# A hybrid encoder layer on one core: the branch product's sums and low halves on VectorE only, the second branch's blocks all ahead of the first branch, two pairs interleaved, the out product opened over seven of eight blocks

## The chip, the cores and the metric

The kernel runs on one core of one Trainium2 chip. The metric is the device time of one execution in microseconds; lower is better. The core's engines are TensorE (PE), VectorE (DVE), ScalarE (ACT), GpSimd (POOL) and SyncE (SP); here SP issues nearly all DMAs, and POOL those that add to memory.

## The reference

One layer of a streaming encoder over 1024 prompt rows and 32 sample rows, in float32. Only the piece between the two branches and the residual is touched: `oa` (1056 rows of 1024) and `ob` (1056 rows of 512) come from the two attention branches, `ga` and `gb` are gates.

```python
h = rms_norm(x, g_pre_mix)
qa, ka, va, ra, alr, qb, kb, vb, ga, gb = split_cols(h @ w_in)
oa, s_gla = gla_branch(qa, ka, va, ra, alr, w_a2, b_a2, g_gla, gla_s0, gla_block)
ob, k_rows, v_rows = attn_fn(qb, kb, vb, rel_bias)
mix = (jax.nn.sigmoid(ga) * (oa @ w_br_a) + jax.nn.sigmoid(gb) * (ob @ w_br_b)) @ w_out
x = x + rms_norm(mix, g_post_mix)
...
```

## The kernel before

Everything is held transposed: a tile has 128 feature rows and up to 1056 tokens (1024 of the prompt and 32 of the sample). The tokens are cut into three chunks of 352 (`chunk(c)`) or two halves of 528 (`one`, `two`). The weights are cut into blocks of 128 by 128.

A product keeps float32 accuracy by splitting each operand into a high half (a copy by ACT into a shorter format) and a low half (the operand less its high half, a subtraction). Each block is then three matmuls: high times high, weight's high times low, weight's low times high. `split_hi_lo` and `split_both` issue the copy on ACT and the subtraction on DVE; `branch_half` does this for half a weight tile (four blocks, 128x512), with the subtraction on POOL (line 1684).

The branch product has two kinds of units. A **branch B unit** (`branch_b(n, c)`) is block n of `ob @ w_br_b` for one chunk, 12 matmuls of 352 columns (lines 231 to 233); its eviction multiplies by the gate row `gb[n]` (line 1721) and the last chunk stores the row to `d_tb[n]`. A **branch A product** (`branch_a(m, n)`) is one of seven products by which a pair m of output blocks (m and m+4) over two halves of inner blocks and two halves of tokens is formed with seven products in place of eight: `a11, s0, s1, s3, s2, a12, a22`, each 24 matmuls of 264 columns (lines 1816 to 1818). Their moving operands are the rows of `oa` or sums of them: `b11`, `b21`, `b22` are parts of the rows and `t1` to `t4` sums, made once by `first_sum` and `third_sum` (POOL) and `t2_sum` and `t4_sum` (DVE) and split by the functions with `_split`. All four pairs use the same operands, so they are made during the first pair. A product accumulates in one of four PSUM pairs `BK`; evictions copy (ACT), add and gate (DVE), and POOL's DMA adds the finished rows to `d_tb` in memory (`add_row`).

The order is the list `seq`: branch B's blocks 4, 5 and 6 (blocks 0 to 3 ran earlier), then pair after pair of branch A with the next pair's a11 ahead of a pair's a12, and branch B's block 7 at the end. The table `work` says which sums and splits are issued with which unit, `at` splits a unit's weights two units ahead. Weights are loaded by SP (`weights_load`, two buffers of two halves each). Rows of gates and products (`ev`) rotate through four buffers (`evt`), so a load into one waits for the store from it to land. PE, DVE and ACT run in the order in which the code issues; POOL's and SP's queues too.

Then `mix @ w_out` opens: rows of `d_tb` are loaded into `ml`, split into `mh` and `ml` (`mix_split`, `mix_last`), and each output block sums eight row blocks in the order `MIX = (0, 4, 1, 5, 2, 6, 3, 7)`. Rows 3 and 7 come straight from the last pair's eviction and from branch B's last block.

Of the kernel before, what the change touches and what calls it, by code (L numbers as in the profile page):

```python
# [18 lines left out]
P = 128  # L19
# [91 lines left out]
B21P = ()  # L111
B22P = ()


def emit(tc, a):
# [1427 lines left out]
    for u in range(16):  # L1543
# [81 lines left out]
        if u == 14:  # L1625
            while fill["at"] < 3 * FIRST:
                piece()
                flush()
            xp.release()
            key_copies(15)  # L1630
            bo = pool("bo", side="right")
            for x in "hl":
                OB[x] = tl(bo, [P, 4, T], F32R, tag="b" + x)
            eb = pool("eb", side="right")
            branch_split(0)
            split_tile()
            load_tile()
            gate_rows(1)
# [31 lines left out]
    XO = {n: [[t[:, h] for t in oa[r + k]] for k in range(HK)] for n, r, h in (("b11", 0, one), ("b21", HK, one), ("b22", HK, two), ("t4", 0, two))}  # L1670
# [4 lines left out]
    def split_both(n, k, t, eng=ve):  # L1675
        ac.activation(XO[n][k][0], t, AF.Copy)
        eng.tensor_tensor(XO[n][k][1], t, XO[n][k][0], op=ALU.subtract)

    wsp = {}

    def branch_half(key, t, eng=po):
        h, l = wsp[key] = [tl(wp, [P, HK, P], F32R, tag=x, bufs=4) for x in ("whi", "wlo")]
        ac.activation(h, t, AF.Copy)
        eng.tensor_tensor(l, t, h, op=ALU.subtract)
# [26 lines left out]
    def branch_b(n, c):  # L1711
        h, l = [t[n % 2] for t in FB] if n < 6 else wsp["b", n]
        s = chunk(c)
        ps = (BK[1 + c % 2][:, 0] if BK else ps_two()[:, 0] if (n, c) == (6, NC - 1) else ps_mm())[:, : s.stop - s.start]
        product(ps, [h], [l], [(k, k) for k in range(HK)], lambda k: OB["h"][:, k, s], lambda k: OB["l"][:, k, s])

        def evac():
            if n == 6 and c == 0:
                gb[n] = evt()
            g = gb[n]  # L1720
            ve.tensor_tensor(g[:, s], ps, (oa[KT - 1][0].bitcast(F32) if n == 6 else g)[:, s], op=ALU.mult)
# [31 lines left out]
    def third_sum(k):  # L1753
        t = thirds[k] = tl(sx, [P, HT], tag="t", bufs=1)
        po.tensor_tensor(t, raw_row(HK + k)[:, two], raw_row(k)[:, two], op=ALU.subtract)

    def b22_split(k):
        split_both("b22", k, raw_row(HK + k)[:, two], po if k in B22P else ve)

# [6 lines left out]
    def b21_split(k):  # L1766
        split_both("b21", k, raw_row(HK + k)[:, one], po if k in B21P else ve)

# [3 lines left out]
    def half_tile():  # L1772
        return tl(sx, [P, HT], tag="n", bufs=4)
# [6 lines left out]
    def pair_load(m):  # L1780
        q = pairs_[m] = Pair()
        q.m, q.x, q.v, q.w = m, BK[0 if m % 2 else 3], BK[2], BK[1]
        q.g = [evt() for i in range(2)]
        q.parts = [t[:, h] for t in (evt(), evt()) for h in (one, two)] if m == 0 else []
        for i in range(2):
            dma.dma_start(q.g[i], d_ga[m + HK * i])
# [20 lines left out]
    def branch_a(m, n):  # L1807
        q = pairs_[m]
# [12 lines left out]
        def evac():  # L1821
            if n in ("a11", "s0", "s1"):
                t = q.parts.pop(0) if q.parts else half_tile()
                setattr(q, n, t)
                ac.activation(v2(t), V if n == "s0" else X, AF.Copy)
            elif n == "s3":
                ve.tensor_tensor(v2(q.s1), V, v2(q.s1), op=ALU.add)
                gated_part(q, 0, two, v2(q.s1), 1)
            elif n == "s2":
                ve.tensor_tensor(v2(q.s0), X, v2(q.s0), op=ALU.add)  # L1830
                gated_part(q, 1, two, v2(q.s0), -1)
            elif n == "a12":
                ve.tensor_tensor(v2(q.a11), W, v2(q.a11), op=ALU.add)
                gated_part(q, 0, one, v2(q.a11), 1)
                if m < HK - 1:
                    add_row(q, 0)
            else:
                gated_part(q, 1, one, X, -1)
                if m < HK - 1:
                    add_row(q, 1)  # L1840
# [4 lines left out]

    def mix_load(c):
        for k in MIX[:-2]:
            dma.dma_start(ml[:, k, chunk(c)].bitcast(F32), d_tb[k, :, chunk(c)])

    def mix_split(k, c):  # L1850
        s = chunk(c)
        split_hi_lo(mh[:, k, s], ml[:, k, s], ml[:, k, s].bitcast(F32))

    def mix_last(n, c):
        s = chunk(c)
        g = pairs_[HK - 1].g[n // HK][:, s]
        ve.tensor_tensor(g, g, (gb[n] if n == KT - 1 else tv)[:, s], op=ALU.add)
        split_hi_lo(mh[:, n, s], ml[:, n, s], g)

    def terms():  # L1860
        tr = pool("tr")
        for n in ("t1", "t2", "t3"):
            XO[n] = [[tl(tr, [P, HT], F32R, tag=f"{n}{k}{x}") for x in "hl"] for k in range(HK)]
        return tr
# [6 lines left out]
    use = {("b", 6): 6, ("b", KT - 1): len(seq) - 3} | {u: i for i, u in enumerate(seq) if u[0] != "b"}  # L1871
# [5 lines left out]
    def split_weights(u):  # L1877
        i = order_w.index(u)
        if i % 2 == 0:
# [4 lines left out]
    work = {0: [(first_sum, 0), (first_sum, 1), (first_split, 0)], 1: [(first_sum, 2), (first_split, 1)], 2: [(first_sum, 3), (first_split, 2)], 3: [(first_split, 3)],  # L1884
            4: [(t1_split, 0)], 5: [(t1_split, 1), (t1_split, 2)], 6: [(t1_split, 3), (t2_sum, 0)], 7: [(third_sum, 0), (t2_sum, 1), (t2_split, 0)],
            8: [(t2_sum, 2), (t2_split, 1), (t3_split, 0), (third_sum, 1)], 9: [(t2_sum, 3), (t2_split, 2), (t2_split, 3), (t3_split, 1), (third_sum, 2)],
            10: [(b22_split, 0), (b22_split, 1), (t3_split, 2), (third_sum, 3), (b22_split, 2)],
            11: [(b22_split, 3), (t3_split, 3), (t4_sum, 0), (b21_split, 0)], 12: [(t4_sum, 1), (b21_split, 1)],
            13: [(t4_sum, 2), (b21_split, 2)], 14: [(t4_sum, 3), (b21_split, 3), (t4_split, 0), (t4_split, 1)], 15: [(t4_split, 2), (t4_split, 3)]}
    tr = mp = None  # L1890
# [3 lines left out]
    def out_halves(n, eng):  # L1894
        raw = tl(wp, [P, KT, P], tag="raw", bufs=2)
        dma.dma_start(raw, a["w_out"][n])
        for i in range(2):
            branch_half(("out", n, i), raw[:, i * HK : i * HK + HK], eng)
            if i == 0:
                yield  # L1900
# [3 lines left out]
    out0, out1 = out_halves(0, po), out_halves(1, ve)  # L1904

    work |= {N - 4: [(mix_split, 0, 0), (mix_split, 4, 0)], N - 3: [(next, out0), (next, out0), (mix_split, 1, 0), (mix_split, 5, 0)],
             N - 2: [(mix_split, 2, 0), (mix_split, 6, 0), (mix_last, HK - 1, 0)], N - 1: [(next, out1)]}
    for i, u in enumerate(seq):
        if i == 4:
            tr = terms()  # L1910
        if i == 9:
            repsum((0, 0, 4))
            BK = [ps_pair() for x in range(4)]
            pair_load(0)
        evac = branch_b(*u[1:]) if u[0] == "b" else branch_a(u[1], u[0])
        if u[0] == "s3":
            if u[1] + 1 < HK:
                pair_load(u[1] + 1)
            else:
                gb[KT - 1], tv = evt(), evt()  # L1920
                dma.dma_start(gb[KT - 1], d_gb[KT - 1])
                dma.dma_start(tv, d_tb[HK - 1])
        if u == ("a22", HK - 1):
            tr.release()
            op.release()
# [3 lines left out]
            for c in range(NC):  # L1929
                mix_load(c)  # L1930
# [4 lines left out]
        if u[0] == "s2":  # L1935
            pair_gate(u[1])
        evac()
    next(out1)
    sx.release()
# [162 lines left out]

    for c in range(NC):
# [3 lines left out]
        for n in range(KT):  # L2107
            hi, lo = wout[n]
            ps = ps_mm()
            product(ps[:, :CW], hi, lo, [(k, k) for k in MIX], lambda k: mh[:, k, s], lambda k: ml[:, k, s])  # L2110
            if c == 0:
                if n == 0:
                    out_weights(2)
                if n < 2:
                    mix_last(HK - 1, 1 + n)
                    mix_last(KT - 1, 1 + n)
                if n == 1:
                    ev.release()
                    bo.release()
# [1008 lines left out]
```

## Time and profile before

| what | us |
|---|---|
| median of 3 runs (lowest, highest) | 1884.36 (1881.78, 1886.1) |
| the profiled execution's own time | 1884.82 |
| span of its records | 1883.1 |
| first matmul of branch B's block 4 | 880.50 |
| first matmul of branch A | 897.98 |
| first matmul of the out product | 999.22 |

Lines of the profile name an engine, a line of the kernel, an operation, its output and input tiles, and the shape. A wait row reads: engine, the waiting tile and line, what released it, the total, the number and the longest. In a timeline the brackets hold the idle time just before an operation and what ended it.

### The profile page before, as it was taken

The page shows a single profiled execution, that of the slowest core. Times are in us where ns is not written, and L with a number is a line of the kernel's source. Part 1 is how long each engine was busy: PE and PEld are TensorE (multiplying, and loading weights), DVE is VectorE, ACT ScalarE, POOL GpSimd, SP SyncE. Part 2 cuts the span into 40 slices and gives each one's busy share as a digit, 9 for nine tenths or more (in the row PEclk, how much of TensorE's full clock was granted, in tenths as well). Part 3 has the DMA queues.
Part 4 walks back from the last instruction along what each step waited for, and adds up shares of the span by engine and source line. Part 5 has one row for each costly group of instructions (what it writes and reads, how often), then busy time and mean ns, then how long its engine had stood idle before and what let it go on. Part 6 is the DMA issues. An engine that isn't in the chain of part 4 may idle for free.

```text
span 1883.1 us, 35213 instructions
## 1 busy us (share of the span) xinstructions
PE 1847.1 (98%) x13808; PEld 1810.0 (96%) x13808; DVE 1278.7 (68%) x2387; ACT 974.8 (52%) x2062; POOL 285.7 (15%) x466
## 2 busy tenths in 40 slices
PE   8999999999999999999899999999999999999997
PEld 8999999999999999999899999999999999999996
DVE  6955543666655766776736776888888876558777
ACT  7545334666666666553525455433333355555555
POOL 0000001131100111102540111111122210000112
PEclk9999999999999999999999999999999999999998
DMA  7222326355534657578575467555557679887746
GB/s 281 84 103 104 114 81 200 96 144 136 124 82 124 171 134 191 166 221 299 166 208 196 143 246 286 182 173 182 177 165 184 165 204 303 279 287 240 237 151 110
DMA packets 129618, 336.00 MB, mean 178 GB/s; under 512 B 15204, under 2 KB 40620, under 8 KB 128812
## 3 DMA queue, kind: packets, MB, share of 16 engines
q1 hardware_dynamic: 92732, 220.74, 35.8%
q0 software_dynamic: 35280, 108.34, 21.9%
q10 hardware_dynamic: 1440, 4.69, 0.6%
q8 instruction: 108, 1.77, 0.4%
q14 instruction: 58, 0.48, 0.1%
HBM read 225.98 MB, written 132.75 MB: 191 GB/s over the span
## 4 chain that ended last, share of the span: by engine, by line
PE 36%; DVE 4%; issue 4%; DMA 3%; ACT 2%; POOL 1%; SPq 0%; POOLq 0%; DVEq 0%; ACTq 0%
PE two L2357 6%; PE two L2355 6%; PE two L2356 6%; PE two L2802 3%; PE two L2800 3%; PE two L2801 3%; PE mm L233 2%; PE mm L231 2%; PE mm L232 2%; DMA raw<-in_w_br_a 1%; PE two L2264 1%; DMA uraw<-d_b 1%; PE two L2266 1%; PE two L2265 1%; DMA d_tb<-ev 0%
## 5 line engine op out<-in xcount | busy, mean ns | idle before, releaser
L824 PE MATMUL mm<-xh,whi 128*128 128x352 f32 x696 | 238.1, 342 | 1.0 <-ACT ev L715 1.0
L826 PE MATMUL mm<-xh,wlo 128*128 128x352 f32 x696 | 225.0, 323 | 0.0
L825 PE MATMUL mm<-xl,whi 128*128 128x352 f32 x696 | 224.6, 323 | 0.0
L2802 PE MATMUL two<-d,wlo 128*128 128x264 f32 x616 | 174.4, 283 | 1.1 <-DVE wlo L2536 1.1
L2801 PE MATMUL two<-d,whi 128*128 128x264 f32 x616 | 174.7, 284 | 0.2 <-DVE d L2487 0.2
L2800 PE MATMUL two<-d,whi 128*128 128x264 f32 x616 | 174.6, 284 | 0.0
L2345 ACT ACTIVATE whi<-ws 128x512 fp32r<-128x512 f32 x88 | 55.5, 631 | 162.0 <-PE two L2356 155.4
L824 PEld LDWEIGHTS mm<-xh,whi 128*128 128x128 f32 x696 | 131.2, 189 | 3.7 <-ACT ev L715 1.3
L825 PEld LDWEIGHTS mm<-xl,whi 128*128 128x128 f32 x696 | 131.2, 189 | 0.3
L826 PEld LDWEIGHTS mm<-xh,wlo 128*128 128x128 f32 x696 | 130.6, 188 | 0.0
L2356 PE MATMUL two<-ml,whi 128*128 128x264 f32 x448 | 126.5, 283 | 0.0
L2357 PE MATMUL two<-mh,wlo 128*128 128x264 f32 x448 | 125.9, 284 | 0.0
L2355 PE MATMUL two<-mh,whi 128*128 128x264 f32 x448 | 125.8, 283 | 0.0
L2802 PEld LDWEIGHTS two<-d,wlo 128*128 128x128 f32 x616 | 116.4, 189 | 1.6 <-DVE wlo L2536 1.6
L2801 PEld LDWEIGHTS two<-d,whi 128*128 128x128 f32 x616 | 115.8, 188 | 0.5 <-DVE d L2487 0.5
L2800 PEld LDWEIGHTS two<-d,whi 128*128 128x128 f32 x616 | 115.7, 188 | 0.0
L961 ACT ACTIVATE s<-s,sm 128x640 f32<-128x640 f32 (+5 forms) x72 | 50.6, 703 | 93.3 <-DVE sm L960 90.5
L237 DVE TENSOR_TENSOR wlo<-raw,whi 128x512 fp32r<-128x512 f32 x80 | 55.8, 702 | 57.5 <-ACT whi L236 52.2
L619 PE MATMUL two<-th,whi 128*128 128x264 f32 x320 | 90.8, 284 | 0.0
L620 PE MATMUL two<-tl,whi 128*128 128x264 f32 x320 | 90.8, 284 | 0.0
L621 PE MATMUL two<-th,wlo 128*128 128x264 f32 x320 | 90.6, 284 | 0.0
L2536 DVE TENSOR_TENSOR wlo<-wraw,whi 128x512 fp32r<-128x512 f32 (+1 forms) x81 | 51.7, 643 | 50.7 <-ACT whi L2535 50.5
(784 smaller groups left out, 6357.9 us busy)
## 6 DMA issues: line engine op xcount, KB each, us to landing
raw<-in_w_in SPq DMA_DIRECT2D x52, 512.0 KB, 3.7
d_b<-av POOLq DMA_DIRECT2D x33, 528.0 KB, 3.5
d_ws<-in_w_down POOLq DMA_DIRECT2D x24, 704.0 KB, 6.6
uraw<-d_b SPq DMA_DIRECT2D x32, 528.0 KB, 5.2
raw<-in_w_up SPq DMA_DIRECT2D x29, 512.0 KB, 4.6
sraw<-in_w_up SPq DMA_DIRECT2D x22, 512.0 KB, 3.6
wraw<-d_ws SPq DMA_DIRECT2D x16, 704.0 KB, 5.7
d_b<-sm POOLq DMA_DIRECT2D x11, 792.0 KB, 6.3
```

What stands on the lines that cost most here:

```text
L619: pe.matmul(ps[:, j, :HC], w[0][:, k], x[0](k, s), start=st, stop=False, skip_group_check=True)
L620: pe.matmul(ps[:, j, :HC], w[0][:, k], x[1](k, s), start=False, stop=False, skip_group_check=True)
L621: pe.matmul(ps[:, j, :HC], w[1][:, k], x[0](k, s), start=False, stop=sp_, skip_group_check=True)
L824: pe.matmul(ps, wh, h[:, k, s], start=(k == 0), stop=False)
L825: pe.matmul(ps, wh, l[:, k, s], start=False, stop=False)
L826: pe.matmul(ps, wl, h[:, k, s], start=False, stop=(k == cnt - 1))
L2355: pe.matmul(ps[:, j, :HC], w[0][:, k], x[0][:, k, s], start=st, stop=False, skip_group_check=True)
L2356: pe.matmul(ps[:, j, :HC], w[0][:, k], x[1][:, k, s], start=False, stop=False, skip_group_check=True)
L2357: pe.matmul(ps[:, j, :HC], w[1][:, k], x[0][:, k, s], start=False, stop=sp_, skip_group_check=True)
L2800: pe.matmul(o, wh, xh_[:, s], start=(k == 0 and p in (0, 4, 5)), stop=False, skip_group_check=True)
L2801: pe.matmul(o, wh, xl_[:, s], start=False, stop=False, skip_group_check=True)
L2802: pe.matmul(o, wl, xh_[:, s], start=False, stop=(k == HD - 1 and p in (3, 4, 6)), skip_group_check=True)
```

## The change

It moves all sums and all low halves of the branch product to DVE; POOL keeps only the DMAs that add to `d_tb`. Branch B's block 7 follows block 6, so that all branch B units stand ahead of branch A; its gate row is loaded at block 6's first eviction. Pairs 0 and 1 of branch A are interleaved, then pair 2 begins inside pair 1's end and pair 3 inside pair 2's; the gate rows of a pair are loaded at the units in `LOADS`, and the sigmoid on them moves from the eviction of s2 to that of s3. Tiles move between pools: the sums' halves get buffers of their own, and six half tiles take the products' parts. Chunk 0 of the rows 0, 4, 1, 5, 2, 6 is loaded into staging tiles during the last pair, and its splits stand around the last product. The first two blocks of the out product each run over seven row blocks, and then the eighth is added to both.

```diff
+            eb = pool("eb", side="right")
             bo = pool("bo", side="right")
...
-            eb = pool("eb", side="right")
...
-    sx = pool("sx", side="right")
-    op = pool("op", side="right")
+    tr = pool("tr")
+    T1 = {n: [[tl(tr, [P, HT], F32R, tag=f"{n}{k}{x}") for x in "hl"] for k in range(HK)] for n in ("t1", "t2", "t3")}
+    op = pool("op")
+    sx = pool("sx")
...
-    def branch_half(key, t, eng=po):
+    def branch_half(key, t):
         h, l = wsp[key] = [tl(wp, [P, HK, P], F32R, tag=x, bufs=4) for x in ("whi", "wlo")]
         ac.activation(h, t, AF.Copy)
-        eng.tensor_tensor(l, t, h, op=ALU.subtract)
+        ve.tensor_tensor(l, t, h, op=ALU.subtract)
...
         def evac():
             if n == 6 and c == 0:
-                gb[n] = evt()
-            g = gb[n]
-            ve.tensor_tensor(g[:, s], ps, (oa[KT - 1][0].bitcast(F32) if n == 6 else g)[:, s], op=ALU.mult)
-            if n == KT - 1:
-                if c == 0:
-                    mix_last(n, 0)
-            elif c == NC - 1:
-                dma.dma_start(d_tb[n], g)
+                gb[6], gb[7] = evt(), evt()
+                dma.dma_start(gb[7], d_gb[7])
+            ve.tensor_tensor(gb[n][:, s], ps, (oa[KT - 1][0].bitcast(F32) if n == 6 else gb[n])[:, s], op=ALU.mult)
+            if c == NC - 1:
+                dma.dma_start(d_tb[n], gb[n])
...
     def first_sum(k):
...
-        po.tensor_tensor(sums[k], r[:, one], r[:, two], op=ALU.subtract)
+        ve.tensor_tensor(sums[k], r[:, one], r[:, two], op=ALU.subtract)
...
     def third_sum(k):
-        t = thirds[k] = tl(sx, [P, HT], tag="t", bufs=1)
-        po.tensor_tensor(t, raw_row(HK + k)[:, two], raw_row(k)[:, two], op=ALU.subtract)
+        t = thirds[k] = tl(hx, [P, HT], tag="t", bufs=2) if k in (1, 2) else tl(sx, [P, HT], tag="t", bufs=1)
+        ve.tensor_tensor(t, raw_row(HK + k)[:, two], raw_row(k)[:, two], op=ALU.subtract)
...
     def half_tile():
-        return tl(sx, [P, HT], tag="n", bufs=4)
+        return tl(hx, [P, HT], tag="half", bufs=6)
...
+    def stage_load(k):
+        n = MIX.index(k)
+        if n % 3 == 0:
+            staged["t"] = tl(hx, [P, T], tag="st", bufs=4)
+        staged[k] = staged["t"][:, CW * (n % 3) : CW * (n % 3 + 1)]
+        dma.dma_start(staged[k], d_tb[k, :, chunk(0)])
...
+    def mix_add(n, c):
+        g = pairs_[HK - 1].g[n // HK][:, chunk(c)]
+        ve.tensor_tensor(g, g, tv[n][:, chunk(c)], op=ALU.add)
...
-    seq = [("b", n, c) for n in (4, 5, 6) for c in range(NC)] + [("a11", 0)]
-    for m in range(HK):
-        seq += [(n, m) for n in NAMES[1:5]] + [("a11", m + 1)] * (m + 1 < HK) + [("a12", m), ("a22", m)]
-    seq += [("b", KT - 1, c) for c in range(NC)]
+    seq = [("b", n, c) for n in (4, 5, 6, 7) for c in range(NC)]
+    seq += [("a11", 0), ("s0", 0), ("a11", 1)] + [(n, m) for m in (0, 1) for n in NAMES[1 + (m == 0) : 5]]
+    seq += [("a12", 0), ("a22", 0), ("a12", 1), ("a11", 2), ("a22", 1)] + [(n, 2) for n in NAMES[1:5]] + [("a11", 3)]
+    seq += [("a12", 2), ("a22", 2)] + [(n, 3) for n in NAMES[1:]]
...
-    work |= {N - 4: [(mix_split, 0, 0), (mix_split, 4, 0)], N - 3: [(next, out0), (next, out0), (mix_split, 1, 0), (mix_split, 5, 0)],
-             N - 2: [(mix_split, 2, 0), (mix_split, 6, 0), (mix_last, HK - 1, 0)], N - 1: [(next, out1)]}
+    work |= {N - 2: [(next, out0), (next, out0)], N - 1: [(mix_split, k, 0) for k in MIX[:4]]}
+    LOADS = {("a11", 0): 0, ("s3", 0): 1, ("s0", 2): 2, ("a11", 3): 3}
...
+        if u == ("s2", HK - 1):
+            for k in MIX[:6]:
+                stage_load(k)
+            tv = {n: tl(hx, [P, T], tag="st", bufs=4) for n in (HK - 1, KT - 1)}
+            for n in tv:
+                dma.dma_start(tv[n], d_tb[n])
...
-            for c in range(NC):
+            for c in (1, 2):
                 mix_load(c)
...
-        if u[0] == "s2":
+        if u[0] == "s3":
             pair_gate(u[1])
         evac()
+    mix_split(MIX[4], 0)
+    mix_add(HK - 1, 0)
+    mix_split(MIX[5], 0)
+    mix_add(KT - 1, 0)
+    mix_last(HK - 1, 0)
     next(out1)
-    sx.release()
+    mix_last(KT - 1, 0)
+    next(out1)
...
+            ps = ps_mm() if (c, n) != (0, 1) else ahead[1][0]
+            if c or n > 1:
+                out_part(ps, hi, lo, MIX)
+            elif n == 0:
+                ahead = [(ps, hi, lo), (ps_mm(), *wout[1])]
+                for x in ahead:
+                    out_part(*x, MIX[:-1])
+                for x in ahead:
+                    out_part(*x, MIX[-1:])
```

Where the change moves instructions, at three places. On **DVE**, from the second chunk of branch B's block 6 on; `ev` is the gated row, `t2`, `t3` and `oa` name the operands' halves, `n` and `t` the sums. Before:

```order
L1721 TENSOR_TENSOR ev_10546<-mm_10548,oa7h_10360 128x352
L1746 SCALAR_TENSOR_TENSOR n_10421<-n_10421,oa6l_10359 128x528
L1677 TENSOR_TENSOR t21l_10475<-n_10403,t21h_10474 128x528
L1677 TENSOR_TENSOR t30l_10481<-t_10565,t30h_10480 128x528
L1721 TENSOR_TENSOR ev_10546<-two_10571,oa7h_10360 128x352
L1746 SCALAR_TENSOR_TENSOR n_10439<-n_10439,oa7l_10361 128x528
L1677 TENSOR_TENSOR t22l_10477<-n_10421,t22h_10476 128x528
L1677 TENSOR_TENSOR t23l_10479<-n_10439,t23h_10478 128x528
L1677 TENSOR_TENSOR t31l_10483<-t_10596,t31h_10482 128x528
L1677 TENSOR_TENSOR oa4l_10355<-oa4l_10355,oa4h_10354 128x528
L1677 TENSOR_TENSOR oa5l_10357<-oa5l_10357,oa5h_10356 128x528
L1677 TENSOR_TENSOR t32l_10485<-t_10649,t32h_10484 128x528
```

After:

```order
L1720 TENSOR_TENSOR ev_10547<-mm_10572,oa7h_10387 128x352
L235 TENSOR_TENSOR t22l_10364<-n_10464,t22h_10363 128x528
L235 TENSOR_TENSOR t23l_10366<-n_10483,t23h_10365 128x528
L1720 TENSOR_TENSOR ev_10548<-mm_10590,ev_10548 128x352
L1683 TENSOR_TENSOR wlo_10625<-raw_10501,whi_10624 128x512
L1751 TENSOR_TENSOR t_10628<-oa4l_10382,oa0l_10390 128x528
L1720 TENSOR_TENSOR ev_10548<-mm_10608,ev_10548 128x352
L1683 TENSOR_TENSOR wlo_10645<-raw_10501,whi_10644 128x512
L235 TENSOR_TENSOR oa4l_10382<-oa4l_10382,oa4h_10381 128x528
L1720 TENSOR_TENSOR ev_10548<-two_10631,ev_10548 128x352
L1683 TENSOR_TENSOR wlo_10696<-raw_10621,whi_10695 128x512
L1751 TENSOR_TENSOR t_10699<-oa5l_10384,oa1l_10392 128x528
```

Weight halves (`wlo`) and the sums `t` now stand between the evictions, and three evictions of block 7 ahead of the halves of `oa5` and of `t3`.

On **SP**, the queue that loads and stores, around the store of branch B's first row (`ev` to `d_tb`); `d_gb` and `d_ga` hold gate rows, `d_wa` and `in_w_br_a` weights. Before:

```order
L808 DMA d_tb_3242<-ev_10041 128x1056
L1700 DMA raw_10501<-d_wa_3253 128x512 x2
L1726 DMA d_tb_3242<-ev_10346 128x1056
L1700 DMA raw_10584<-d_wa_3253 128x512 x2
L1726 DMA d_tb_3242<-ev_10347 128x1056
L1786 DMA ev_10608<-d_ga_961 128x1056
L1786 DMA ev_10609<-d_ga_961 128x1056
L1726 DMA d_tb_3242<-ev_10546 128x1056
L1700 DMA raw_10676<-in_w_br_a 128x512 x2
```

After:

```order
L806 DMA d_tb_3242<-ev_10041 128x1056
L1699 DMA raw_10501<-in_w_br_a 128x512
L1699 DMA raw_10501<-d_wa_3253 128x512
L1722 DMA d_tb_3242<-ev_10346 128x1056
L1719 DMA ev_10548<-d_gb_962 128x1056
L1722 DMA d_tb_3242<-ev_10347 128x1056
L1699 DMA raw_10621<-in_w_br_a 128x512
L1699 DMA raw_10621<-d_wa_3253 128x512
L1784 DMA ev_10688<-d_ga_961 128x1056
L1722 DMA d_tb_3242<-ev_10547 128x1056
L1784 DMA ev_10689<-d_ga_961 128x1056
```

The load of gate row 7 from `d_gb` now stands between the first two stores of branch B, ahead of the second pair of weight loads for branch A, and the first two loads of gates are no longer side by side.

On **DVE** again, from the gating of the last pair's a12 up to the weights of the out product's second block; `two` is the PSUM of the last product, `st` a staging tile. Before:

```order
L1799 TENSOR_TENSOR ev_11224<-n_11299,ev_11224 128x528
L237 TENSOR_TENSOR ml_11552<-ml_11552,mh_11553 128x352 x2
L1797 SCALAR_TENSOR_TENSOR ev_11225<-two_10604,ev_11225 128x528
L237 TENSOR_TENSOR ml_11552<-ml_11552,mh_11553 128x352 x2
L1721 TENSOR_TENSOR ev_11452<-two_10605,ev_11452 128x352
L1857 TENSOR_TENSOR ev_11225<-ev_11225,ev_11452 128x352
L237 TENSOR_TENSOR ml_11552<-ev_11225,mh_11553 128x352
L237 TENSOR_TENSOR ml_11552<-ml_11552,mh_11553 128x352 x2
L1857 TENSOR_TENSOR ev_11224<-ev_11224,ev_11453 128x352
L237 TENSOR_TENSOR ml_11552<-ev_11224,mh_11553 128x352
L1721 TENSOR_TENSOR ev_11452<-two_10606,ev_11452 128x352
L1684 TENSOR_TENSOR wlo_11642<-raw_11639,whi_11641 128x512
```

After:

```order
L1797 TENSOR_TENSOR ev_11345<-half_11353,ev_11345 128x528
L235 TENSOR_TENSOR ml_11621<-st_11537,mh_11622 128x352 x3
L235 TENSOR_TENSOR ml_11621<-st_11541,mh_11622 128x352
L1795 SCALAR_TENSOR_TENSOR ev_11346<-two_10660,ev_11346 128x528
L235 TENSOR_TENSOR ml_11621<-st_11541,mh_11622 128x352
L1865 TENSOR_TENSOR ev_11345<-ev_11345,st_11545 128x352
L235 TENSOR_TENSOR ml_11621<-st_11541,mh_11622 128x352
L1865 TENSOR_TENSOR ev_11346<-ev_11346,st_11546 128x352
L235 TENSOR_TENSOR ml_11621<-ev_11345,mh_11622 128x352
L1683 TENSOR_TENSOR wlo_11655<-raw_11652,whi_11654 128x512
L235 TENSOR_TENSOR ml_11621<-ev_11346,mh_11622 128x352
L1683 TENSOR_TENSOR wlo_11661<-raw_11652,whi_11660 128x512
```

Block 7's evictions (into `ev` from `two`, 352 columns) have gone from here, four splits stand ahead of the last product's gating (the 128x528 operation on `two`), and the two halves of the second block's weights stand behind the splits of rows 3 and 7.

More of the change, by code (lines that the diff above doesn't have):

```diff
@@ L110 @@
 CVS = 0
-B21P = ()
-B22P = ()
 def emit(tc, a):
@@ L1766, in b21_split @@
     def b21_split(k):
-        split_both("b21", k, raw_row(HK + k)[:, one], po if k in B21P else ve)
+        split_both("b21", k, raw_row(HK + k)[:, one])
     def t4_split(k):
@@ L2101, in up_split, with out_part @@
             wup[i, p] = h, l
+    def out_part(ps, hi, lo, ks):
+        product(ps[:, :CW], hi, lo, [(k, k) for k in ks], lambda k: mh[:, k, s], lambda k: ml[:, k, s], first=ks[0] == MIX[0], last=ks[-1] == MIX[-1])
     for c in range(NC):
```

82 lines of the change are left out of this document (36 added, 46 removed).

## The prediction

> **What bounds the kernel now.** I read the page's span and busy lines first, to see which engine a gain has to come from.
>
> ```profile
> span 1883.1 us, 35213 instructions
> ...
> PE 1847.1 (98%) x13808; PEld 1810.0 (96%) x13808; DVE 1278.7 (68%) x2387; ACT 974.8 (52%) x2062; POOL 285.7 (15%) x466
> ```
>
> PE is the bound, so the change is worth what PE now loses in the stage that it touches. I then cut that stage into windows that begin and end at a first matmul: eight units of branch B, the eight products of branch A up to the second pair's a11, the other twenty products of branch A, and branch B's block 7 up to the first matmul of the out product. The columns are the stretch, its length, the busy time of PE, PE's weight loads, DVE, ACT and POOL, the granted PE clock, the DMA share and GB/s.
>
> ```profile
> 880.50:896.03 15.53, 15.53 (x98) 15.53 (x97) 12.18 (x19) 5.84 (x11) 6.45 (x6) 1.00 1.03 405
> 897.98:930.84 32.86, 27.55 (x193) 26.14 (x193) 28.91 (x31) 17.97 (x31) 17.22 (x12) 0.90 0.36 124
> 930.84:989.83 58.99, 58.77 (x482) 58.55 (x481) 16.83 (x21) 17.74 (x29) 28.85 (x24) 1.00 0.79 212
> 989.83:999.22 9.39, 7.56 (x39) 7.27 (x38) 6.51 (x11) 4.62 (x11) 2.81 (x2) 0.82 0.99 340
> ```
>
> Rows one and three are undisturbed and give the price of a unit: 15.53/8 = 1.94 us for a branch B unit and 58.99/20 = 2.95 us for a branch A product. At these prices row two should last 8 × 2.95 = 23.6 us and lasts 32.86, a loss of 9.26; row four should last 3 × 1.94 = 5.82 and lasts 9.39, a loss of 3.57. Together **12.8 us** are lost. In row two DVE is busy 28.91 of 32.86 us: it sets the pace there. The waits of PE over the stage (total, times, longest) name it too:
>
> ```profile
> PE two L1817 <- DVE oa7l L1677: 2.3, 1, 2.3
> PE two L231 <- DVE ev L1721: 1.8, 1, 1.8
> PE two L1817 <- DVE oa3l L1677: 1.1, 1, 1.1
> PE two L1817 <- DVE oa2l L1677: 1.0, 1, 1.0
> PE two L1817 <- DVE oa6l L1677: 0.6, 1, 0.6
> PE two L1816 <- ACT ev L1825: 0.3, 1, 0.3
> PE two L1818 <- POOL wlo L1684: 0.2, 1, 0.2
> ```
>
> These are 7.3 us, nearly all for low halves that DVE made late. The other 5.5 us are slow matmuls behind the two long waits, as the timeline of PE and a finer cut show:
>
> ```profile
> 912.45 0.42 PE L1818 MATMUL two<-oa7h,wlo 128*128 128x264 f32 x1
> 912.67 0.42 PE L1816 MATMUL two<-oa4h,whi 128*128 128x264 f32 x1
> ...
> 929.38 0.28 PE L1816 MATMUL two<-oa0h,whi 128*128 128x264 f32 x1
> 929.50 0.28 PE L1817 MATMUL two<-oa0l,whi 128*128 128x264 f32 x1
> ...
> 995.70 0.49 PE L231 MATMUL two<-bh,whi 128*128 128x352 f32 x1 [1.83 <-DVE ev L1721]
> 995.99 0.49 PE L232 MATMUL two<-bl,whi 128*128 128x352 f32 x1
> ...
> 999.44 0.32 PE L232 MATMUL mm<-ml,whi 128*128 128x352 f32 x1
> 999.60 0.32 PE L233 MATMUL mm<-mh,wlo 128*128 128x352 f32 x1
> ```
> ```profile
> 910.00:920.00 10.00, 7.93 (x45) 7.93 (x46) 9.40 (x10) 8.27 (x13) 6.00 (x5) 0.66 0.33 105
> 920.00:930.00 10.00, 7.87 (x61) 7.24 (x60) 8.60 (x11) 3.23 (x6) 4.28 (x3) 1.00 0.35 108
> ```
>
> After the 2.3 us wait matmuls start 0.22 us apart instead of 0.12 at a granted clock of 0.66; after the 1.83 us wait 0.29 instead of 0.16. After the waits of 1.0 and 1.1 us the clock stayed at 1.00. So a wait of about 1 us costs itself, and one of 1.8 us costs about 1.6 us more (12 matmuls, 0.13 each). The Trainium skill (TensorE: Matmul & The Clock Gate, "What's actually happening") has the clock halved only after an idle window of some 3.4 us; the trace disagrees, since 1.83 us sufficed. By that rule a new stall of 2 us would cost 2 us, by the trace 3.6; I price stalls by the trace.
>
> **Why DVE is late.** The timeline of DVE and POOL, and the group of POOL's weight halves:
>
> ```profile
> 899.42 0.70 DVE L1677 TENSOR_TENSOR t30l<-t,t30h 128x528 fp32r<-128x528 f32 x1
> 900.04 0.51 DVE L1721 TENSOR_TENSOR ev<-two,oa7h 128x352 f32<-128x352 f32 x1
> 900.47 1.61 DVE L1746 SCALAR_TENSOR_TENSOR n<-n,oa7l 128x528 f32<-128x528 f32 x1
> ...
> 910.25 1.76 DVE L1677 TENSOR_TENSOR oa7l<-oa7l,oa7h 128x528 fp32r<-128x528 f32 x1 [1.20 <-POOL t L1755]
> ```
> ```profile
> 900.19 1.32 POOL L1755 TENSOR_TENSOR t<-oa5l,oa1l 128x528 f32<-128x528 f32 x1 [1.26 <-DVE t30l L1677]
> 910.18 1.26 POOL L1684 TENSOR_TENSOR wlo<-raw,whi 128x512 fp32r<-128x512 f32 x1
> ```
> ```profile
> L1684 POOL TENSOR_TENSOR wlo<-raw,whi 128x512 fp32r<-128x512 f32 x32 | 44.5, 1404 | 49.0 <-ACT whi L1683 42.2 <-PE two L1817 6.8
> 1000.10 0.68 DVE L1684 TENSOR_TENSOR wlo<-raw,whi 128x512 fp32r<-128x512 f32 x1
> 1000.70 0.52 DVE L1721 TENSOR_TENSOR ev<-two,ev 128x352 f32<-128x352 f32 x1
> ```
>
> Alone a 128x528 operation of DVE has 0.70 us and the next starts 0.62 later; an eviction of 352 columns takes a step of 0.43; a weight half takes a step of 0.60 on DVE and 1.40 us on POOL. Beside a POOL operation DVE's own grow to 1.61 and 1.76: each overlap costs DVE about 1 us. In row two above, 31 operations at about 0.70 would be 21.7 us and DVE was busy 28.91: 7 us of sharing.
>
> **The change, part by part.**
>
> *All sums and halves on DVE.* POOL loses 8 sums and 32 weight halves, DVE gains them and no longer shares. Branch B's twelve units: 22 operations × 0.62 + 12 evictions × 0.43 + 4 weight halves × 0.60 = 21.2 us of DVE beside 12 × 1.94 = 23.3 us of PE. The first ten branch A products: 22 × 0.62 + 10 × 0.60 + 8 evictions' operations at about 0.72 = 25.4 us beside 29.5. DVE fits in both, thinly in the first. Walking DVE's queue in order against PE's, with block 7 ending at 903.8: the weight half of the first a11 is ready at about 901.2 (read at 903.5), the last b22 half at 910.5 (read at 915.2), the last b21 half at 927 (932.7). The nearest is 2.3 us early. So the waits of row two go, and the half clock with them: **+9.3 us**.
>
> *Block 7 of branch B ahead of branch A.* Its three units cost PE 5.82 us as before but no longer sit at the end with an eviction, an addition and a split behind them: **+3.6 us**. What is late next is the last product's eviction.
>
> *Two pairs interleaved.* The PE work is the same 28 products. It gives the sums two more products before each new operand is read, which is where the margins above come from; alone nothing.
>
> *Out product over seven of eight blocks.* Between the last matmul of a22 of pair 3 and its row's low half stand on DVE the eviction, four splits and sums, and the split itself.
>
> ```profile
> L1797 DVE SCALAR_TENSOR_TENSOR ev<-two,ev 128x528 f32<-128x528 f32 x4 | 2.8, 706 | 2.9 <-PE two L1818 2.9
> 996.83 0.53 DVE L237 TENSOR_TENSOR ml<-ev,mh 128x352 fp32r<-128x352 f32 x1 [0.62 <-ACT mh L236]
> ```
>
> Counting from the last product's end: eviction done at 0.9, then four operations of 352 columns at about 0.45 to 2.7, row 3's low half at 3.25, half a weight at 3.85, row 7's low half and the second weight half at 5.0. PE takes 3 × 0.16 = 0.48 a block and wants row 3 at 2.9 and that last weight half at 4.5: waits of about 0.2, 0.4 and 0.5, in all **−1.0 to −1.5 us**. Without the opening over seven blocks PE would want row 7 at 7 × 0.48 = 3.4 and not after n = 1's seven blocks: some 1 us more.
>
> *DMA.* Gate row 7 is now loaded at block 6's first eviction, into a tile that the store issued at 882.91 frees; the staged rows are six small loads behind the accumulating stores. The rows are that issue, the landing times of the plain stores up to 905 us and those of the accumulating ones.
>
> ```profile
> 882.91 0.32 SPq L808 DMA_DIRECT2D d_tb<-ev  x1
> ...
> DMA to landing us min/median/max: 3.6/7.2/10.3
> ```
> ```profile
> L1802 POOL DMA_DIRECT2D d_tb<-ev x6: 834/884/1154, 931.0 to 974.2; - x6
> ...
> DMA to landing us min/median/max: 3.6/8.7/10.2
> ```
>
> At the median landing the tile is free at 890.1, and the row is read at 880.5 + 10 × 1.94 = 899.9: of the loads themselves no row stands here, so I take the stores' landings. The median (7.2) hides it, the longest (10.3) costs nothing yet, as DVE has 2.3 us to spare. The accumulating stores land 8.7 to 10.2 us after issue; weights queued behind them have about 14 (below). I cost both at nothing; the bound if cover goes is in the rivals.
>
> **Sum.** 9.26 + 3.57 − 1.0 to 1.5 = 11.3 to 11.8. Counting a product at 24 matmuls × 0.122 = 2.93 instead of 2.95 adds 28 × 0.02 = 0.6. I take 12.0. The profiled run took 1884.82 us (span 1883.1 and 1.7 around it), so 1872.8; that run is 0.46 above the median of 1884.36, so **1872.5**.
>
> **Rivals.**
>
> *DVE is the bound in branch B's last units.* For it: only 2.1 us of cover in 23.3. An operation that needs the one ahead of it steps 0.7 or more, since it waits for the whole 0.70; were all 26 at 0.75, DVE would be 3.4 us later, PE would stall 1 to 3 us at the first a11 and pay up to 1.6 for the clock: 1874 to 1877. The same price if gate row 7 takes more than about 12 us to land (899.9 + 2.3 − 890.1), in a stretch where DMA share is 1.03: each us beyond costs one, since DVE's queue stands still behind that eviction.
>
> *The change does not do what it says.* If it was ACT's high halves and not POOL that made DVE late (the wait ahead of 996.83 is ACT's), row two's loss stays, and only 3.6 − 1.2 is gained, less what waits anew: 1881 to 1883. Against it: the two longest stalls end on operations of 1.76 us and on a wait for POOL itself.
>
> *Slower: weights behind accumulating stores.* For pairs 2 and 3 the gate rows and staged rows wait in SP's queue for an accumulating store of the pair two before, and weights stand behind them. First place: the store issues at the eviction of pair 0's a12, 903.8 + 11 × 2.95 + 1.6 = 937.9; the weights behind it feed pair 2's s2, whose matmuls start at 903.8 + 18 × 2.95 = 956.9, with a split of 1.3 us ahead, and take 3.7 to land (row below): 956.9 − 1.3 − 3.7 − 937.9 leaves the store about 14 us.
>
> ```profile
> raw<-in_w_in SPq DMA_DIRECT2D x52, 512.0 KB, 3.7
> ```
>
> There are four such places. Beyond 14 us each costs the excess, and 1.6 us of clock once that reaches 1.8. To turn 12 us gained into over 3.8 lost each place must lose 4.0, that is 2.4 + 1.6: landings of about 16.4 us, giving 1889 or more. The longest seen is 10.2. The Trainium skill (SBUF — State Buffer, "Who interferes with whom") says a busy DVE can starve GpSimd's making of descriptors, but not through tensor_tensor, which takes only the read side of the shared port; no run here shows it yet.
>
> **How the numbers follow.** Forecast (1870 to 1874.5) 0.62; DVE or gate row late (1874.5 to 1880.6) 0.24; no more than the tail gained (1880.6 to 1888) 0.08; slower 0.06. About 0.2%, or 3.8 us, is what a measurement of this kernel can tell from no change; so faster 0.86, same 0.08, slower 0.06. The range runs from 1869.0 (no wait at the opening, 13.4 gained, and 2 us of the runs' own spread) to 1879.0, which takes in the first rivals' prices.
>
> **What would show it.** Right: between the first branch B unit and the first out matmul about 106 us instead of 118.7, PE clock at 1.00 throughout, no DVE operation of 528 columns over 0.8 us, short waits for ml and wlo at the opening. Wrong: a PE wait for wlo of the first a11; a DVE wait for a DMA at block 7's eviction; ACT waiting for weights in pairs 2 and 3.

## The result and the profile after

The changed kernel takes 1871.09 us (median of 4 runs, 1869.19 to 1873.01) against 1883.43 before: a ratio of 0.9933, 95% interval 0.9916 to 0.995, so 12.3 us faster. Five more runs gave 1871.92 beside 1885.02 (0.9933, 0.992 to 0.9945). The prediction was 1872.5 in a range of 1869.0 to 1879.0.

The page after opens with these lines; DVE does more than before, POOL less, and PE idles less.

```profile
span 1867.5 us, 35190 instructions
...
PE 1840.5 (99%) x13808; PEld 1805.9 (97%) x13808; DVE 1288.2 (69%) x2427; ACT 975.1 (52%) x2062; POOL 227.5 (12%) x426
```

The stage cut as in the prediction's table, with the same columns: branch B's twelve units, the first ten branch A products, the other eighteen, and the first 10 us of the out product.

```profile
878.84:902.14 23.30, 23.30 (x145) 23.30 (x145) 22.16 (x38) 9.35 (x16) 0.00 (x0) 1.00 1.00 382
902.14:931.30 29.16, 29.16 (x242) 29.16 (x241) 24.44 (x39) 19.68 (x33) 0.00 (x0) 1.00 0.44 150
931.30:983.97 52.67, 52.67 (x434) 52.63 (x433) 27.94 (x44) 18.13 (x31) 5.11 (x6) 1.00 0.85 244
983.97:993.97 10.00, 9.65 (x60) 9.08 (x59) 9.19 (x20) 5.61 (x12) 0.00 (x0) 1.00 1.04 370
```

PE is busy for the whole of the first three rows, at full clock: **105.13 us** from the first branch B matmul to the first out matmul, where before had 118.72. That is 13.6 of the 15.63 us by which the two profiled executions differ. Another 1.66 us lie ahead of the stage (it begins at 878.84, before at 880.50) and are no part of the change: the instructions there are the same, and in later runs of the new order the stage began anywhere from 879.0 to 881.7 us. The stage's 13.6 less the 0.8 that the opening loses (below) is 12.8; the medians differ by 12.3. The last 1.2 us of the 15.63 lie behind the first two out blocks, where this profile has 875.0 us to the end and before had 876.2; the other profiles of the new order have 875.0 to 877.2, so this too is scatter.

At the opening PE still waits twice, in these rows of its timeline (the bracket holds the wait and what ended it):

```profile
986.85 0.32 PE L229 MATMUL mm<-mh,whi 128*128 128x352 f32 x1
987.27 0.43 PE L230 MATMUL mm<-ml,whi 128*128 128x352 f32 x1
...
988.35 0.32 PE L230 MATMUL mm<-ml,whi 128*128 128x352 f32 x1
988.91 0.43 PE L231 MATMUL mm<-mh,wlo 128*128 128x352 f32 x1 [0.24 <-DVE wlo L1683]
```

Matmuls of 352 columns follow each other by 0.16 us. Row 3's low half costs 0.42 − 0.16 = 0.26 here, the second block's last weight half 0.56 − 0.16 = 0.40. From the first out matmul to the third block's first are 8.55 us, where before had 7.73.

### The profile page after: what moved, and what is told of

The parts are those of the page before. It is cut to its first block, busy times and chain, and to the rows that moved or that the text cites. A ratio compares the mean times of both kernels' runs of the same rounds, so it can differ in the third digit from the quotient of the medians.

```text
span 1867.5 us, 35190 instructions
## 1 busy us (share of the span) xinstructions
PE 1840.5 (99%) x13808; PEld 1805.9 (97%) x13808; DVE 1288.2 (69%) x2427; ACT 975.1 (52%) x2062; POOL 227.5 (12%) x426
## 4 chain that ended last, share of the span: by engine, by line
PE 65%; DVE 3%; ACT 2%; issue 1%; DMA 0%; SPq 0%; DVEq 0%; ACTq 0%
PE two L2380 6%; PE two L2378 6%; PE two L2379 6%; PE mm L822 4%; PE mm L824 4%; PE mm L823 4%; PE mm L231 3%; PE mm L229 3%; PE mm L230 3%; PE two L2825 3%; PE two L2823 3%; PE two L2824 3%; PE two L2287 2%; PE two L2289 2%; PE two L2288 2%; PE two L1818 1%
```

## The experiments

The prediction's theory: POOL's operations stretch DVE's, DVE is therefore late in the first pair, and moving all of it to DVE cures that. Its rival: the order does it, since block 7 ahead and the interleaving give DVE's work more time before it is read, whoever does it. Each run is compared with runs of the kernel before on the same chip.

**The old order, all on DVE.** The kernel before with the engine changed and nothing else:

```diff
-    def branch_half(key, t, eng=po):
+    def branch_half(key, t, eng=ve):
...
-        po.tensor_tensor(sums[k], r[:, one], r[:, two], op=ALU.subtract)
+        ve.tensor_tensor(sums[k], r[:, one], r[:, two], op=ALU.subtract)
...
-        po.tensor_tensor(t, raw_row(HK + k)[:, two], raw_row(k)[:, two], op=ALU.subtract)
+        ve.tensor_tensor(t, raw_row(HK + k)[:, two], raw_row(k)[:, two], op=ALU.subtract)
...
-    out0, out1 = out_halves(0, po), out_halves(1, ve)
+    out0, out1 = out_halves(0, ve), out_halves(1, ve)
```

> The kernel before, its order untouched, with its 8 sums and 32 weight halves of the branch product moved from POOL to DVE. Sharing theory (a POOL operation that runs beside a DVE operation adds about 1 us to it, and that is why DVE is late): between the first branch A matmul and the second pair's t10 DVE has 31 + 12 = 43 operations at 0.62, 26.7 us, so the stretch falls from 32.86 to about 26 to 28 us, and the stretch of block 7 at the end stays at 9.4. Time 1876 to 1879. Order theory (it matters where block 7 and the first pair's sums stand, not which engine does them): DVE, busy 28.91 of 32.86 us there, gets 12 more operations; the stretch grows to 35 us or more and the time is that of before or some us longer.

1879.7 us beside 1885.11: ratio 0.9976 (0.9965 to 0.9987), 5.4 us faster. The windows from the first branch A matmul to the second pair's t10 and of block 7 at the end, and PE's waits from 895 to 1000 us:

```profile
898.08:927.11 29.03, 25.14 (x194) 23.72 (x193) 27.60 (x44) 18.45 (x32) 0.21 (x1) 1.00 0.46 153
985.62:993.15 7.53, 6.07 (x38) 5.78 (x37) 5.53 (x12) 4.20 (x9) 0.00 (x0) 1.00 0.97 327
```
```profile
PE two L1817 <- DVE oa7l L1677: 2.5, 2, 1.9
PE two L231 <- DVE ev L1721: 1.5, 1, 1.5
PE two L1817 <- DVE oa6l L1677: 0.6, 1, 0.6
PE two L1817 <- DVE oa2l L1677: 0.4, 1, 0.4
PE two L1816 <- ACT ev L1825: 0.4, 1, 0.4
```

DVE does 44 operations in less time than 31 took before (27.60 against 28.91 us): the sharing is real, and ending it takes 3.8 us from the first pair and 1.9 from block 7. Much of that is the clock and not the waiting. In the first pair the granted clock rises from 0.90 to 1.00 and PE's busy time for the same products falls by 2.4 us (27.55 to 25.14), its idle time by 1.4 (5.31 to 3.89); in block 7 the busy time falls by 1.5 (7.56 to 6.07) and the idle time by 0.4. The longest waits are still there: 1.9 us where before had 2.3, and 1.5 for block 7's eviction where before had 1.8. DVE is still busy 27.60 of 29.03 us and PE still waits for it: the engine alone does not cure the first pair in the old order. The 26 to 28 us expected for the stretch were too little by 1, the 1876 to 1879 for the time by 0.7, and block 7's stretch did not stay at 9.4.

**The new order, with POOL doing its old share**, in whole or in part (of the 32 weight halves the 30 of the branch product; the out product's two stay on DVE). The parts, as edits to the changed kernel (the whole is both):

```diff
-        ve.tensor_tensor(l, t, h, op=ALU.subtract)
+        (ve if key[0] == "out" else po).tensor_tensor(l, t, h, op=ALU.subtract)
```
```diff
-        ve.tensor_tensor(sums[k], r[:, one], r[:, two], op=ALU.subtract)
+        po.tensor_tensor(sums[k], r[:, one], r[:, two], op=ALU.subtract)
...
-        ve.tensor_tensor(t, raw_row(HK + k)[:, two], raw_row(k)[:, two], op=ALU.subtract)
+        po.tensor_tensor(t, raw_row(HK + k)[:, two], raw_row(k)[:, two], op=ALU.subtract)
```

> The changed kernel with the branch product's weight halves back on POOL (those of the out product stay on DVE). Sharing theory: in the first ten branch A products DVE loses 10 operations of 0.6 and has about 10 others stretched by 1 us each, so about 29 of 29.5 us: PE waits of 1 to 4 us in all there, DVE operations of 1.6 to 1.8 us beside POOL's, none later; 1 to 5 us above the changed kernel. Order theory: within 1 us of the changed kernel, stretch of the branch product 105 to 106 us.

> The changed kernel with only the 8 sums (first and third) back on POOL. Sharing theory: 8 stretches of about 1 us against 8 x 0.62 saved, net 2 to 3 us more of DVE time, half of it in branch B's units where DVE has 2 us to spare: PE waits 0 to 2 us in all. Order theory: no wait. The two differ little here; the run bounds what the sums alone are worth.

> The changed kernel with both the 8 sums and the 30 branch weight halves back on POOL: the new order and the new opening alone. If the order by itself already takes the first pair off the critical path (as the two runs with one of the groups on POOL suggest): the first ten branch A products at full rate (29.2 us), DVE busy 27 to 28 us of them, the stage 106 to 107.5 us, then a late w_out and a wait of about 2 us with a slow clock at the opening, as with the halves alone: 1875 to 1878. If sharing and late sums still add up: PE waits of 2 us or more for low halves in the first pair, the stage over 109 us, 1879 or more.

Halves on POOL: 1876.4 (ratio to before 0.9954, 0.9939 to 0.9969). Sums on POOL: 1870.49 (0.9924, 0.9909 to 0.9939), the same as the changed kernel. Both: 1876.88 (0.9957, 0.9942 to 0.9972). The first ten products in the run with both:

```profile
903.35:932.51 29.16, 29.16 (x241) 29.16 (x241) 25.97 (x26) 19.68 (x33) 20.04 (x14) 1.00 0.52 167
```

PE is busy throughout at full clock, as in the changed kernel, with POOL busy 20 us beside DVE; from the first branch A matmul to the third pair's t10, fifteen products, both traces have 43.8 us (903.35 to 947.10 and 902.14 to 945.90). **The order alone takes the first pair off the critical path**; there it no longer matters that POOL does its old share. ("The order" is here all of the change but the engine: block 7 ahead, the interleaving, the new buffers and the opening.) What the halves on POOL cost lies later. In the run with the halves alone the stage is 106.83 us (1.7 more) and the first two out blocks take 11.62 (3.1 more); with the sums as well 107.70 and 11.61. The timelines of POOL, SP, ACT and PE with the halves alone, and then the rows of POOL and SP in the changed kernel:

```profile
966.64 3.75 POOL L1683 TENSOR_TENSOR wlo<-raw,whi 128x512 fp32r<-128x512 f32 x3 [4.63 <-ACT whi L1682]
970.34 1.73 POOL L1800 DMA_DIRECT2D d_tb<-ev  x2
...
980.17 0.87 SPq L1901 DMA_DIRECT2D raw<-in_w_out  x2
...
984.37 1.15 ACT L1682 ACTIVATE whi<-raw 128x512 fp32r<-128x512 f32 x2 [7.87 <-DMA raw<-in_w_out]
...
988.18 0.43 PE L230 MATMUL mm<-ml,whi 128*128 128x352 f32 x1 [1.79 <-DVE ml L235]
```
```profile
965.58 0.84 POOL L1800 DMA_DIRECT2D d_tb<-ev  x1 [17.41 <-DMA raw<-d_wa]
...
973.42 0.33 SPq L1901 DMA_DIRECT2D raw<-in_w_out  x1
```

The accumulating stores of pair 2 stand in POOL's queue behind weight halves, which wait for a high half, which waits for a weight load. The first of them issues 91.2 us after the stage's begin instead of 86.7. SP's loads of the staged rows wait for them to land, the load of `w_out` stands behind those (issued at 980.17 instead of 973.42), and at the opening ACT and then PE wait. Within pair 2 PE also waits once, 0.8 us, for a weight half from POOL. To test where the cost lies, only the halves needed before the first accumulating store went to POOL:

```diff
-        ve.tensor_tensor(l, t, h, op=ALU.subtract)
+        (po if use.get(key, 99) < 22 else ve).tensor_tensor(l, t, h, op=ALU.subtract)
```

> The changed kernel with the weight halves on POOL for the units up to the first two pairs' s2 (14 halves), on DVE from the first a12 on, when the accumulating stores begin. If the 5 us that the halves on POOL cost come from the accumulating stores that stand behind late weight halves in POOL's queue (issued 970.3 there, 965.6 and 967.8 with the halves on DVE), and so from w_out loaded 7 us later: nothing of it here, the stage 105 to 105.7 us, waits at the opening under 1 us, the time within 1 us of the changed kernel, 1870 to 1872.5. If they come from DVE operations stretched beside POOL in the first pair: most of it stays, 1874 or more.

1870.48 us (0.9921, 0.9904 to 0.9938), the changed kernel's time; the stage 105.20, the first two out blocks 8.56. So the cost comes from the later halves. The run does not part their two ways to cost time, the stores held in POOL's queue and the weights that come late; that most goes through the stores is read from the timelines. (It moved 12 halves, not the 14 that the expectation counts.) The group of one of the operand rows in its first ten products, count, total and mean in ns:

```profile
L235 DVE TENSOR_TENSOR oa5l<-oa5l,oa5h 128x528 fp32r<-128x528 f32 x2 | 3.2, 1588 | 1.6 <-ACT oa5h L234 1.6
```

DVE's operations are stretched to 1.6 us there, and it costs nothing, since the new order has room for it.

**POOL busy with work that nobody reads**, beside all on DVE:

```diff
         ve.tensor_tensor(l, t, h, op=ALU.subtract)
+        if key[0] != "out":
+            x, y = [v.rearrange("p k c -> p (k c)") for v in (t, h)]
+            for i in (0, 192, 320):
+                po.tensor_tensor(tl(sx, [P, 192], F32R, tag="dummy", bufs=1), x[:, i : i + 192], y[:, i : i + 192], op=ALU.subtract)
```

> The changed kernel, and POOL besides computes each branch weight half's low half a second time, in three pieces, into a tile that nobody reads. Nothing waits for POOL's result. Sharing theory: each of these stretches DVE operations by about 1 us in all, so DVE needs 21 + 4 = 25 us in branch B's 23.3 and 25 + 10 = 35 in the first ten products' 29.5: PE waits 5 to 8 us and pays 1.6 to 4 us for the clock, 6 to 12 us above the changed kernel. If instead only POOL's lateness as a producer mattered: within 1 us of the changed kernel.

1886.48 us, the time of the kernel before (1.0006, 0.9997 to 1.0016): all that the change gains is lost, some 14 us by the ratios. Two groups of the stretch from 878 to 996 us, and three windows: the first ten products, the next two, and a stretch of pair 2:

```profile
L1687 POOL TENSOR_TENSOR dummy<-raw,whi 128x192 fp32r<-128x192 f32 x90 | 77.6, 863 | 57.7 <-ACT whi L1682 45.4 <-issue 6.3
...
L1683 DVE TENSOR_TENSOR wlo<-raw,whi 128x512 fp32r<-128x512 f32 x32 | 28.4, 890 | 24.8 <-ACT whi L1682 24.7
```
```profile
902.31:934.26 31.95, 29.46 (x241) 29.25 (x241) 31.78 (x34) 19.38 (x32) 28.55 (x32) 1.00 0.40 132
934.26:943.76 9.50, 6.96 (x50) 6.05 (x49) 9.40 (x12) 2.42 (x4) 7.18 (x9) 1.00 0.21 72
959.92:971.15 11.23, 9.10 (x63) 8.88 (x61) 5.78 (x8) 4.11 (x6) 6.88 (x9) 0.85 1.04 373
```

In the first two windows DVE is busy 31.78 of 31.95 and 9.40 of 9.50 us: here sharing does make it the bound. They last 6.4 us longer than in the changed kernel (29.17 and 5.85 there). In most of the rest DVE is not the bound: the third window is 3.9 us longer (7.30 there) with DVE busy for half of it, and the first two out blocks take 11.57 us, as with the halves on POOL. The whole is more than the 6 to 12 us expected. Three pieces take 2.6 us of POOL for each half (77.6/30) where one operation took 1.4; they hold the weight buffers longer (SP waits 10.6 us for them in all), and the accumulating stores stand behind them too. The run shows that a POOL operation costs DVE time without its result being awaited; its size is not that of the kernel before, and DVE is full in stretches that account for 6.4 us of it.

**The pairs one after another**, with the sums and splits moved up to the deadlines that this gives:

```diff
-    seq += [("a11", 0), ("s0", 0), ("a11", 1)] + [(n, m) for m in (0, 1) for n in NAMES[1 + (m == 0) : 5]]
-    seq += [("a12", 0), ("a22", 0), ("a12", 1), ("a11", 2), ("a22", 1)] + [(n, 2) for n in NAMES[1:5]] + [("a11", 3)]
-    seq += [("a12", 2), ("a22", 2)] + [(n, 3) for n in NAMES[1:]]
+    seq += [("a11", 0)]
+    for m in range(HK):
+        seq += [(n, m) for n in NAMES[1:5]] + [("a11", m + 1)] * (m + 1 < HK) + [("a12", m), ("a22", m)]
...
-    LOADS = {("a11", 0): 0, ("s3", 0): 1, ("s0", 2): 2, ("a11", 3): 3}
+    LOADS = {("a11", 0): 0, ("s3", 0): 1, ("s3", 1): 2, ("s3", 2): 3}
```

> The changed kernel with the pairs one after another as before (the next pair's a11 ahead of a12), the sums and splits moved up to their new deadlines. Between branch B and the first a12 DVE then has 18 operations x 0.62 + 6 x 0.60 + 4 x 0.72 = 17.6 us in 6 x 2.93 = 17.6 us of PE, starting 0.6 us late: PE waits of 1 to 3 us in all for b21 and t4 low halves, and up to 1.6 us of clock; the stage 106 to 109 us. If interleaving is worth nothing: 105.1 us.

1874.73 us (0.9946, 0.9931 to 0.9961); the stage 107.59. PE's waits in the stage, and the window around them:

```profile
PE two L1819 <- DVE oa6l L235: 1.0, 1, 1.0
PE two L1819 <- DVE oa7l L235: 0.8, 1, 0.8
```
```profile
920.00:930.00 10.00, 8.20 (x64) 7.67 (x63) 9.71 (x17) 4.41 (x8) 0.90 (x1) 1.00 0.15 53
```

As expected: DVE is full and b21's low halves come late. Interleaving is worth 2.5 us of the stage; the first two out blocks take 0.7 us more as well (9.29), whose cause stays open.

**The first out block over all eight rows at once**:

```diff
-            ps = ps_mm() if (c, n) != (0, 1) else ahead[1][0]
-            if c or n > 1:
-                out_part(ps, hi, lo, MIX)
-            elif n == 0:
-                ahead = [(ps, hi, lo), (ps_mm(), *wout[1])]
-                for x in ahead:
-                    out_part(*x, MIX[:-1])
-                for x in ahead:
-                    out_part(*x, MIX[-1:])
+            ps = ps_mm()
+            out_part(ps, hi, lo, MIX)
```

> The changed kernel with the out product's first block over all eight row blocks at once. In the changed kernel row 7's low half is ready 4.3 us after the first out matmul and would be wanted at 3.6: PE waits 0.6 to 0.9 us there, and 0.4 less for the second block's weight half. Net 0.2 to 0.6 us longer, not to be told apart in the times. If the opening over seven blocks were worth what I put it at (1 us more): 0.6 to 1.0.

1872.35 us (0.9935, 0.992 to 0.995). The first two out blocks take 8.60 us, against 8.55 and 8.57 in the two profiles of the changed kernel: the opening over seven blocks is worth nothing that shows, less than I expected either way. Row 7's wait takes the place of the weight half's:

```profile
990.51 0.43 PE L230 MATMUL mm<-ml,whi 128*128 128x352 f32 x1 [0.29 <-DVE ml L235]
```

**Another order at the opening**, and the changed kernel again beside it:

```diff
-    work |= {N - 2: [(next, out0), (next, out0)], N - 1: [(mix_split, k, 0) for k in MIX[:4]]}
+    work |= {N - 2: [(next, out0), (next, out0)], N - 1: [(mix_split, k, 0) for k in MIX[:6]] + [(mix_add, HK - 1, 0), (mix_last, HK - 1, 0)]}
...
-    mix_split(MIX[4], 0)
-    mix_add(HK - 1, 0)
-    mix_split(MIX[5], 0)
-    mix_add(KT - 1, 0)
-    mix_last(HK - 1, 0)
     next(out1)
-    mix_last(KT - 1, 0)
     next(out1)
+    mix_add(KT - 1, 0)
+    mix_last(KT - 1, 0)
```

> The changed kernel with DVE's and ACT's work at the opening reordered: all six staged rows' splits and row 3's addition and split ahead of the last product's gating, then the second block's weight halves, then row 7's addition and split. Row 3 is wanted 2.9 us after the first out matmul and would be ready before it, the last weight half 3.8 us after it and is wanted at 4.5: the two waits at the opening (0.27 and 0.40 us) go and none comes, 0.6 us from the first out matmul to the third block's first. The times differ by less than they scatter. If DVE's longer queue ahead of the gating holds up the second block's PSUM bank instead: a wait of 0.5 us or more at the second block.

> The changed kernel as it is, beside the run above on the same chip: 1870 to 1872.5, a stage of 105.1 us and waits of 0.6 to 0.7 us at the opening, as in its first profile; and the time up to branch B's block 4 shows how much of the first profile's 1.66 us gain ahead of the stage is scatter (none of it is the change's, if the order up to there is the same).

1870.98 (0.9928, 0.9915 to 0.9942) and 1871.92: not told apart. The first two out blocks take 8.34 us instead of 8.57, less than half of the 0.6 expected, and the stage ahead of them 105.42 instead of 105.11, so nothing is won; the wait for row 3 is gone, one of 0.3 us for a weight half stays. No version here beats the changed kernel.

## Why the prediction was right, point by point

- **What was lost before, 12.8 us, and that it would all come back**: right. The stage fell by 13.6, 0.8 more, since an undisturbed product takes 81.83/28 = 2.92 us and not 2.95.
- **All sums and halves on DVE, +9.3 us**: the gain came, its reason was wrong. The step said that with the sharing gone the waits of the first pair go. In the old order ending the sharing gives 3.8 us of those 9.3, and 2.4 of these are the clock; in the new order the first pair runs at full rate with POOL's work back on POOL. It is the order that took it off the path; that this is block 7's three units and the interleaving ahead of each deadline is argued, as only the interleaving was taken out alone. What DVE adds in the new order it adds elsewhere: 1.7 to 2.6 us in the stage and 3.1 at the opening, by keeping POOL's queue free for the accumulating stores. So the 9.3 us came in full because the same change holds the new order, which is luck as far as this step's argument goes. The prediction had that mechanism as its slower rival for landings, not for issues behind weight halves.
- **Block 7 ahead, +3.6 us**: consistent with the traces (its units run at 1.94 us, and no eviction of branch B stands at the opening); it was not tried alone. In the old order 1.7 us of that loss stay with all on DVE (7.53 − 5.82). The prediction took nearly all of the 7.3 us of waits to be for low halves; 1.83 of them, at 995.70, were for block 7's eviction, and that wait still lasts 1.5 us with POOL idle, so most of it was not sharing.
- **Interleaving, "alone nothing"**: it has no term, though the margins behind the +9.3 were laid to it. Without it, and with everything on DVE, 2.5 us of the stage are lost, so that much belongs to it.
- **Opening, −1.0 to −1.5**: measured 0.85 above the undisturbed 16 × 0.48 = 7.7, at two of the three places named. That seven blocks save 1 us more was wrong: 0.05.
- **DMA at nothing**: right. The accumulating stores landed 7.0 to 8.8 us after issue (before 6.7 to 10.2 by their own line; the view in the prediction, from 3.6, holds a plain transfer too). The gate row was issued at 889.56 and landed 7.1 us later, as a row of SP's timeline and the view of the tensor that it comes from show; DVE read it at 898.59 without a wait (DVE's timeline).

```profile
889.56 0.32 SPq L1719 DMA_DIRECT2D ev<-d_gb  x1
```
```profile
DMA to landing us min/median/max: 7.1/7.1/7.1
```
```profile
898.59 0.51 DVE L1720 TENSOR_TENSOR ev<-mm,ev 128x352 f32<-128x352 f32 x1
```

- **Rivals**: DVE in branch B's units came near (22.16 of 23.30 us) and cost nothing. Of the transfers to and from `d_tb` from 905 to 990 us none landed later than 10.9 us after issue, and ACT did wait for weights in pairs 2 and 3, at most 3.2 us, none of which reached PE. That was named as a sign of being wrong, and here it was none; the signs of being right all came, no DVE operation of 528 columns over 0.8 us among them. The rule of the Trainium skill weighed there (SBUF — State Buffer, "Who interferes with whom") held in so far as POOL's accumulating DMAs still took 0.84 to 0.89 us to issue beside a busier DVE, 0.83 to 1.15 before.

The four corners, as ratios to before: DVE alone 0.9976, order alone 0.9957, both 0.9933, which is their product (the corner of the order alone leaves the out product's two halves on DVE). They seem to add up, but for different reasons: DVE's part comes from the first pair and block 7 in the old order, from POOL's queue and the opening in the new one.

## What to carry to other kernels

When two engines slow each other, look for the place where that is on the critical path: giving the late work more time before its deadline can remove the whole loss, and then it no longer matters who does it. A DMA on a compute engine's queue is as late as the operation queued ahead of it (4.5 us here); follow the wait from store to load to the next stage's weights. A change of two parts is read only by undoing each part alone.

## What was not expected of the hardware

A PE wait of 1.89 us in the old order with all on DVE left the granted clock at 1.00 (the window from 898.08, above), while waits of 0.45 and 1.79 us within 2.7 us, with the halves on POOL, brought 0.83 over the 10 us from the end of the first wait, in matmuls 0.29 apart that began 1.2 us after the second had ended:

```profile
985.97:995.97 10.00, 8.21 (x38) 7.76 (x39) 9.94 (x20) 5.30 (x12) 0.00 (x0) 0.83 0.88 296
```

0.83 is half speed for 3.4 us, the same as behind block 7's wait before (0.82 of 9.39 us) and at the opening with POOL busy for nobody (0.83 of 10 us). So the prediction's price of 1.6 us for a wait of 1.8 is not certain to be charged. The Trainium skill (TensorE: Matmul & The Clock Gate, "What's actually happening") gives a window of about 3.4 us that runs free of the kernel; the length agrees, that a whole window must be idle does not.
